# A down projection that takes some of its K tiles two by two by Strassen's scheme

## The chip, the core and the metric

The kernel runs on one core of one Trainium2 chip. TensorE (PE, its weight loads PEld), VectorE (DVE), ScalarE (ACT), GpSimd (POOL) and the DMA queues that SyncE (SP), ACT and POOL issue work side by side and wait for each other by semaphores. The metric is the device time of one execution in microseconds (us); what counts is the median of several runs.

## The reference, cut to what matters

One layer of a diffusion backbone over 256 latent tokens of width 2048 in float32: modulation, a gated linear attention beside a differential attention, a gated merge, and a gated MLP. The change lies in the last product of the MLP and in the residual that follows it.

```python
def conv_ffn(h, w_up, conv_w, conv_b, w_down):
    u = h @ w_up
    ...
    gate, val = jnp.split(u, 2, axis=-1)
    return (jax.nn.silu(gate) * val) @ w_down
...
    x_new = x_new + g2 * conv_ffn(h2_l, w_up, conv_w, conv_b, w_down)
```

`w_down` is 5632 x 2048. The gate `g2` is one vector of 2048, a part of `silu(c) @ w_ada + b_ada`.

## The kernel before

Each float32 operand of a product is split in two parts, hi (rounded to the type that TensorE takes) and lo (the rest); a product is hi x hi + lo x hi + hi x lo, three matmuls into one bank. Weights arrive as 512 KB tiles in `raw` buffers, of which there are four (`fetch`). `split` makes 512 columns of hi by a copy on ACT (`whi`) and of lo by a subtraction on DVE (`wlo`); there are four hi and four lo buffers, so ACT writes a hi when TensorE has left the one four splits earlier. While the up product runs, each fourth lo is made by POOL; in the down product all are DVE's.

The up product makes 44 tiles `g` (`gs[k]`, 128 channels x 256 tokens, lo in `[:, 0]`, hi in `[:, 1]`), each followed by a convolution, silu and gate on ACT and DVE (`gated`). Beside it runs the rest of the modulation vector as dot products on DVE: `ada_next` loads rows of `w_ada` into `araw` (two buffers) and dots them with `cb`, at a pace of so many per up tile; `ada_done(48)` adds up the gate `g2`.

The down product has 256 tokens x 2048 columns. It is made in two halves of 1024 columns (h = 0, 1); a half fills four banks of 128 tokens x 512 columns (t = 0, 1 and n = 0, 1). For each of 44 K tiles k, `pieces(k)` loads 128 x 1024 weights and splits them in two, and `part` does three matmuls for each of the four banks: 12 matmuls per tile and half, 1056 in all, tied in one order. The first half takes the banks named acc, which the up product used last, the second the banks named aux. The last two tiles of the second half are done bank by bank, so that the banks end one after the other.

Between the tiles stand the steps for the residual (`residual`): `gate_line` and a shuffle spread the gate over the partitions into `cb` (POOL DMAs, two shuffles of 1024 columns on DVE); `turn` turns the residual from channels-by-tokens to tokens-by-channels (four transposes on DVE into `turned`, then 32 small POOL DMAs into `row`, four times); `done` multiplies a bank by the gate, adds the row and stores it (two operations on DVE, a store from ACT's queue). `done` for the first half runs in the second.

A scheduler decides the order on each engine: it places instructions by its own costs and may move a step many tiles ahead of where it is written. What one engine does is then in that fixed order, whatever it waits for.

Of the kernel before, what the change touches and what calls it, by code (L numbers as in the profile page):

```python
# [9 lines left out]
F32 = mybir.dt.float32  # L10
F32R = mybir.dt.float32r
# [3 lines left out]
ALU = mybir.AluOpType  # L15
# [3 lines left out]
P = 128  # L19
D = 2048  # L20
T = 256
# [7 lines left out]
FT = FF // P  # L29
# [9 lines left out]
SWW = 32 + C0 + (NGK + 1) * P  # L39
UPS = 6  # L40
CONVS = 7
SLOTS = 12
EARLY_ADA = 4, 14
GATE_ADA = [0.25] * 4 + [0.5] * 16 + [1] * 12
# [102 lines left out]
def layer_kernel(tc, I, out):  # L147
# [3 lines left out]
    with es:  # L151
# [41 lines left out]
        chain = []  # L193
# [31 lines left out]
        def fetch(src, n):  # L225
            raw = st.tile([P, 1024], F32, tag="raw", bufs=4, name="wraw")
            nc.sync.dma_start(raw[:, :n], src)
# [117 lines left out]
        with tc.tile_pool(name="first", bufs=1) as p1:  # L345
# [188 lines left out]
            ws = sweep_splits(0, lows)  # L534
# [663 lines left out]
        with tc.tile_pool(name="ffn", bufs=1) as pf:  # L1198
# [49 lines left out]

            splits[1] = 0
# [15 lines left out]
            def turn(m):  # L1265

                rows.append([hp.tile([P, 512], F32, tag=f"a{4 * t + m}", name="row") for t in range(2)])
                turned = st.tile([P, 1024], F32, tag="araw", bufs=2, name="turned").rearrange("p (c t) -> p c t", c=4)
                for c in range(4):
                    V.transpose(turned[:, c, :], x1[4 * m + c])  # L1270
                for p in range(4):
                    for q in range(8):
                        to = rows[m][q // 4].rearrange("p (c n) -> p c n", c=4)
                        nc.gpsimd.dma_start(to[32 * (q % 4):32 * (q % 4 + 1), :, 32 * p:32 * (p + 1)],  # L1274
                                            turned[32 * p:32 * (p + 1), :, 32 * q:32 * (q + 1)])

            def residual(h, k):

                if (h, k) == (0, 2):
                    V.transpose(gt, adav[:, 32:64])  # L1280
                elif (h, k) in ((0, 3), (0, 4)):
                    lines.append(gate_line(k - 3))
                elif (h, k) in ((0, 14), (0, 15)):
                    V.stream_shuffle(cb[:, 1024 * (k - 14):1024 * (k - 13)], lines[k - 14], [0] * 32)
                elif (h, k) in ((0, 16), (0, 17), (1, 2), (1, 3)):
                    turn(len(rows))
                elif h and 8 <= k < 12:
                    done(0, k % 2, k // 2 % 2)

            lines = []  # L1290
# [6 lines left out]
            def part(t, n, k, w):  # L1297
                ts = slice(t * P, (t + 1) * P)
                g = gs[k]
                for a, b in ((1, 0), (0, 0), (1, 1)):  # L1300
                    i = PE.matmul(banks[h][t][n], g[:, a, ts], w[n][b], start=k == 0 and (a, b) == (1, 0),  # L1301
                                  stop=k == FT - 1 and b == 1)
                    if chain:
                        after(i, chain[0])
                    chain[:] = [i]

            def done(h, t, n, cols=slice(0, 512)):

                o = slice(1024 * h + 512 * n + cols.start, 1024 * h + 512 * n + cols.stop)
                y = hp.tile([P, 512], F32, tag=f"a{8 + (4 * h + 2 * t + n + (cols.start > 0)) % 8}", name="y")[:, :cols.stop - cols.start]  # L1310
                V.tensor_tensor(y, banks[h][t][n][:, cols], cb[:, o], op=ALU.mult)
                V.tensor_tensor(y, y, rows[2 * h + n][t][:, cols], op=ALU.add)
                nc.scalar.dma_start(out[t * P:(t + 1) * P, o], y)

            banks = []
            for h in range(2):
                banks.append([[acc_bank("down") if h == 0 else aux_bank("down", t) for n in range(2)] for t in range(2)])
                last = FT - 2 if h else FT
                for k in range(last):
                    w = pieces(k)  # L1320
                    for n in range(2):
                        for t in range(2):
                            part(t, n, k, w)
                    residual(h, k)

            ws = [pieces(k) for k in range(last, FT)]
            for n in range(2):
                for t in range(2):
                    for k in range(last, FT):
                        part(t, n, k, ws[k - last])  # L1330
# [17 lines left out]
```

## Time and profile before

| | |
|---|---|
| median of 3 runs | 1698.1 us (1697.58 to 1699.21) |
| the profiled execution | 1699.43 us, span 1697.4 us |
| TensorE busy | 1675.4 us (99%) |
| VectorE, ScalarE, GpSimd busy | 1272.3 us (75%), 980.0 us (58%), 329.7 us (19%) |
| weights of the down product | 88 loads of 512 KB, median 4.2 us from issue to landing |
| down product | from 1448.9 us to the end of the span, 1056 matmuls |

The rows of the profile name a line, an engine, an operation and "out<-in"; `xN` counts instructions. A figure in brackets behind an instruction of the timeline is the idle time of its engine before it, with what ended it. A matmul's own duration overlaps the next one's, so its rate is read from start to start.

### The profile page before, as it was taken

How to read it: one execution, taken by the hardware profiler on the slowest of the kernel's cores; microseconds unless marked ns; L12 is line 12 of the kernel's file. 1: busy time of each engine (PE TensorE's matmuls, PEld its weight loads, DVE VectorE, ACT ScalarE, POOL GpSimd, SP SyncE). 2: the span in 40 equal slices, each digit the busy share in tenths (PEclk: the TensorE clock that was granted, in tenths of full speed). 3: DMA queues.
4: the chain of work that ended last, by engine and by line, in shares of the span. 5: the costliest groups of instructions: out<-in, count | busy, mean ns of one | idle time of the engine just before them, and what ended most of it. 6: DMA issues, size and time to landing. Idle time of an engine off the chain costs nothing.

```text
span 1697.4 us, 28584 instructions
## 1 busy us (share of the span) xinstructions
PE 1675.4 (99%) x10108; PEld 1445.0 (85%) x10108; DVE 1272.3 (75%) x2426; ACT 980.0 (58%) x1984; POOL 329.7 (19%) x431
## 2 busy tenths in 40 slices
PE   7999999999999999999999999999999999999998
PEld 5779899998787888888888998888888888788887
DVE  5556765767688888788988797787888787755655
ACT  5324554756355777666766686666666666444443
POOL 0000213131210000001223200222222222594000
PEclk9999999999999999999999999999999999999999
DMA  9996532434566555688787566676767676676664
GB/s 383 408 408 192 164 127 90 139 110 156 180 208 226 174 187 187 206 283 275 264 265 261 181 199 217 217 240 223 237 227 236 223 239 228 196 225 203 221 192 143
DMA packets 110830, 370.82 MB, mean 218 GB/s; under 512 B 14432, under 2 KB 19552, under 8 KB 110688
## 3 DMA queue, kind: packets, MB, share of 16 engines
q1 hardware_dynamic: 102112, 362.51, 63.7%
q10 hardware_dynamic: 4032, 4.37, 0.8%
q0 software_dynamic: 4544, 2.14, 0.6%
q8 instruction: 79, 1.29, 0.3%
q14 instruction: 63, 0.52, 0.1%
HBM read 364.73 MB, written 2.10 MB: 216 GB/s over the span
## 4 chain that ended last, share of the span: by engine, by line
PE 93%; DVE 4%; DMA 2%; ACT 1%; issue 1%; DVEq 0%; ACTq 0%
PE down L1301 14%; PE upg L262 9%; PE upv L262 9%; PE gate L262 7%; PE sweep L350 5%; PE upg L264 5%; PE upv L264 4%; PE gate L264 4%; PE mix L262 4%; PE ab L350 2%; PE mix L264 2%; DMA araw<-in_w_ada 2%; PE pgb L262 2%; PE pga L262 2%; PE dk L313 2%; PE dk L315 2%
## 5 line engine op out<-in xcount | busy, mean ns | idle before, releaser
L206 ACT CAST whi<-wraw 128x512 fp32r<-128x512 f32 (+2 forms) x1004 | 606.8, 608 | 396.8 <-DVE wlo L213 112.3
L213 DVE TENSOR_TENSOR wlo<-wraw,whi 128x512 fp32r<-128x512 f32 (+2 forms) x932 | 637.3, 692 | 232.9 <-ACT whi L206 221.7
L262 PE MATMUL upg<-a,whi 128*128 128x512 f32 x656 | 229.0, 391 | 0.0
L262 PE MATMUL upv<-a,whi 128*128 128x512 f32 x656 | 229.0, 391 | 0.0
L1301 PE MATMUL down<-whi,g 128*128 128x512 f32 x704 | 218.1, 391 | 2.2 <-DVE C L274 2.2
L264 PE MATMUL upv<-a,wlo 128*128 128x256 f32 x656 | 182.8, 280 | 0.0
L264 PE MATMUL upg<-a,wlo 128*128 128x256 f32 x656 | 182.6, 280 | 0.0
L262 PE MATMUL gate<-a,whi 128*128 128x512 f32 x512 | 180.5, 398 | 0.7 <-ACT whi L206 0.7
L213 POOL TENSOR_TENSOR wlo<-wraw,whi 128x512 fp32r<-128x512 f32 x72 | 100.3, 1393 | 387.9 <-ACT whi L206 383.7
L338 DVE CUSTOM_DVE_ANT_0 araw<-araw,cb 128x1024 f32<-128x1024 f32 x128 | 159.7, 1249 | 12.5 <-DMA araw<-in_w_ada 12.4
L1301 PEld LDWEIGHTS down<-whi,g 128*128 128x128 f32 x704 | 132.7, 189 | 30.3 <-DVE C L274 2.6
L262 PEld LDWEIGHTS upv<-a,whi 128*128 128x128 f32 x656 | 122.4, 187 | 26.6
L262 PEld LDWEIGHTS upg<-a,whi 128*128 128x128 f32 x656 | 122.4, 187 | 26.5
L264 PE MATMUL gate<-a,wlo 128*128 128x256 f32 x512 | 140.4, 284 | 0.0
L1301 PE MATMUL down<-wlo,g 128*128 128x512 f32 x352 | 137.5, 391 | 0.0
L264 PEld LDWEIGHTS upv<-a,wlo 128*128 128x128 f32 x656 | 123.9, 189 | 0.5
L264 PEld LDWEIGHTS upg<-a,wlo 128*128 128x128 f32 x656 | 123.9, 189 | 0.5
L262 PEld LDWEIGHTS gate<-a,whi 128*128 128x128 f32 x512 | 94.4, 188 | 20.5 <-ACT whi L206 1.0
L264 PEld LDWEIGHTS gate<-a,wlo 128*128 128x128 f32 x512 | 96.5, 189 | 6.2 <-issue 1.8
L262 PE MATMUL mix<-a,whi 128*128 128x512 f32 x256 | 88.8, 396 | 0.0
L1301 PEld LDWEIGHTS down<-wlo,g 128*128 128x128 f32 x352 | 66.5, 189 | 13.8
L1274 POOL DMA_DIRECT2D row<-turned x128 | 69.3, 550 | 32.4 <-DVE turned L1270 18.3
(351 smaller groups left out, 3401.6 us busy)
## 6 DMA issues: line engine op xcount, KB each, us to landing
wraw<-in_w_up SPq DMA_DIRECT2D x164, 512.0 KB, 4.4
araw<-in_w_ada SPq DMA_DIRECT2D x128, 512.0 KB, 5.0
wraw<-in_w_down SPq DMA_DIRECT2D x88, 512.0 KB, 4.2
ada<-in_w_ad SPq DMA_DIRECT2D x64, 512.0 KB, 10.0
wraw<-in_w_gate SPq DMA_DIRECT2D x64, 512.0 KB, 4.1
wraw<-in_w_in SPq DMA_DIRECT2D x58, 512.0 KB, 4.0
wraw<-in_w_proj SPq DMA_DIRECT2D x32, 512.0 KB, 4.6
wraw<-in_w_out SPq DMA_DIRECT2D x32, 512.0 KB, 4.4
```

Source lines behind the costliest of these rows:

```text
L206: copied[0] = S.copy(hi[:, :n], raw)
L213: i = e.tensor_tensor(lo[:, :n], raw, hi[:, :n].bitcast(F32), op=ALU.subtract)
L262: i = PE.matmul(b.rearrange("p (a b) -> p a b", a=2), whi[:, sl], acts[k], start=first, stop=last)
L264: i = PE.matmul(b[:, T:], wlo[:, sl], acts[k][:, 1, :], start=False, stop=last)
L313: PE.matmul(o, whi[:, sl], hi[k], start=first and j == 0, stop=False)
L315: i = PE.matmul(o, wlo[:, sl], hi[k], start=False, stop=last and j == 1)
L338: i = V.tensor_tensor_reduce(raw, raw, cb[:, q * 1024:(q + 1) * 1024], 1.0, 0.0, op0=ALU.mult, op1=ALU.add, accum_out=ada2[:, j, q:q + 1])
L350: return kept(PE.matmul(*args, **kw))
L1274: nc.gpsimd.dma_start(to[32 * (q % 4):32 * (q % 4 + 1), :, 32 * p:32 * (p + 1)], turned[32 * p:32 * (p + 1), :, 32 * q:32 * (q + 1)])
L1301: i = PE.matmul(banks[h][t][n], g[:, a, ts], w[n][b], start=k == 0 and (a, b) == (1, 0), stop=k == FT - 1 and b == 1)
```

## The change

In four pairs of K tiles (8 and 9, 14 and 15, 20 and 21, 26 and 27) the four blocks of tokens x columns are made with seven products for eight. The tokens (two blocks of 128) and the two tiles of the pair make a 2 x 2 matrix of blocks on the left, the two tiles and the two blocks of 512 columns one on the right. `left` makes four sums of g blocks (S1 to S4), and splits them; it is done once, in the first half, and kept in `shi` and `slo` for the second. `right` loads the pair's two weight tiles three tiles ahead and makes four sums t on DVE. `seven` splits three weight blocks and the four t, and does seven times three matmuls: three products go straight to banks of the half (`own`), four to the other set of banks (p1, p5, p6, p7), where they add up over the four pairs. Three tiles after the last pair `add_others` sums those four banks to what each block is still owed, and `done` adds it. In the second half `prepared` has multiplied that by the gate and added the row before, so that `done` needs two operations there, as it did.

Besides: the first half now accumulates in the aux banks and keeps the acc banks for the four products, the second half the other way round. All four turns stand in the first half (written at tiles 1, 2, 24 and 25), the gate lines at its end (36, 37), the shuffles at tiles 0 and 1 of the second half, `done(0)` at 2 to 5. The dot products beside the up product are paced to end three tiles earlier.

```diff
+PAIRS = [8, 14, 20, 26]
...
-                    ada_next(32 / (FT - CONVS))
+                    ada_next(32 / (FT - CONVS - 3))
...
+            def left(k):
+                i = PAIRS.index(k)
+                g, h = [gs[q].bitcast(F32) for q in (k, k + 1)]
+                ...
+                V.tensor_tensor(x[:, 0], g[:, :, two], h[:, :, two], op=ALU.add)
+                V.tensor_tensor(x[:, 1], x[:, 0], g[:, :, one], op=ALU.subtract)
+                V.tensor_tensor(y[:, 0], g[:, :, one], g[:, :, two], op=ALU.subtract)
+                V.tensor_tensor(y[:, 1], h[:, :, one], x[:, 1], op=ALU.subtract)
+                ...
+                for j, z in enumerate((x, y)):
+                    V.tensor_tensor(z[:, :, 0, :], z[:, :, 0, :], z[:, :, 1, :], op=ALU.add)
+                    split_act(hi[:, 2 * j:2 * j + 2], lo[:, 2 * j:2 * j + 2], z[:, :, 0, :])
+                return hi, lo
+            def right(k):
+                b1, b2 = [fetch(I["w_down"][h, q], 1024) for q in (k, k + 1)]
+                t = [hp.tile([P, 512], F32, tag=f"c{j}", name=f"t{j + 1}") for j in range(4)]
+                V.tensor_tensor(t[0], b1[:, 512:], b1[:, :512], op=ALU.subtract)
+                V.tensor_tensor(t[1], b2[:, 512:], t[0], op=ALU.subtract)
+                V.tensor_tensor(t[2], b2[:, 512:], b1[:, 512:], op=ALU.subtract)
+                V.tensor_tensor(t[3], b2[:, :512], t[1], op=ALU.subtract)
+                return b1[:, :512], b2[:, :512], b2[:, 512:], t
+            def product(b, a, w, first, last):
+                for x, y in ((0, 0), (1, 0), (0, 1)):
+                    i = PE.matmul(b, a[x], w[y], start=first and (x, y) == (0, 0), stop=last and y == 1)
+                    ...
+            def seven(k, ws):
+                first, last = k == PAIRS[0], k == PAIRS[-1]
+                b11, b21, b22, t = ws
+                S_ = [[q[:, j, :] for q in lefts[k]] for j in range(4)]
+                own, (p1, p5), (p6, p7) = banks[h], *others[h]
+                for b, a, w in ((p1, whole(0, k), b11), (own[0][0], whole(0, k + 1), b21), (own[0][1], S_[3], b22),
+                                (p5, S_[0], t[0]), (p7, S_[2], t[2]), (p6, S_[1], t[1]), (own[1][0], whole(1, k + 1), t[3])):
+                    mine = b in (p1, p5, p6, p7)
+                    product(b, a, split(w, 512), mine and first, mine and last)
+            def add_others():
+                ...
+                S.copy(c11, p1)
+                V.tensor_tensor(both, p6, c11, op=ALU.add)
+                V.tensor_tensor(c12, p5, both, op=ALU.add)
+                V.tensor_tensor(c21, p7, both, op=ALU.add)
+                V.tensor_tensor(c22, p5, c21, op=ALU.add)
+            def prepared(t, n):
+                r = adds[1][t][n]
+                V.tensor_tensor(r, r, cb[:, columns(1, n)], op=ALU.mult)
+                V.tensor_tensor(r, r, rows[2 + n][t], op=ALU.add)
...
             def done(h, t, n, cols=slice(0, 512)):
+                if h == 0:
+                    V.tensor_tensor(y, b, r, op=ALU.add)
+                    V.tensor_tensor(y, y, cb[:, o], op=ALU.mult)
+                    V.tensor_tensor(y, y, rows[n][t], op=ALU.add)
+                else:
+                    V.tensor_tensor(y, b, cb[:, o], op=ALU.mult)
+                    V.tensor_tensor(y, y, r, op=ALU.add)
...
+                if h == 0 and k + 5 in PAIRS:
+                    lefts[k + 5] = left(k + 5)
+                if k + 3 in PAIRS:
+                    rights[k + 3] = right(k + 3)
...
-                banks.append([[acc_bank("down") if h == 0 else aux_bank("down", t) for n in range(2)] for t in range(2)])
+                sets = [[[acc_bank("down") for n in range(2)] for t in range(2)],
+                        [[aux_bank("down", t) for n in range(2)] for t in range(2)]]
+                banks.append(sets[1 - h])
+                others.append(sets[h])
```

Where the instructions stand now is shown at three places on DVE. In the rows, `C` are tiles of the up product on their way through the convolution (`upv`, `upg` its banks), `x` and `slo` belong to left, `t` to right, `araw` and `ada` to the dot products, and line numbers of the new kernel are one higher above the down product.

DVE at the end of the up product and the start of the down product; the `wlo` behind the transposes, below, is the first of the down product. Before:

```order
L338 ISA ada_77 128x1
L232 TENSOR_TENSOR g_16522<-C_7240,g_16522 128x256
L274 TENSOR_TENSOR C_7556<-upg,C_7556 128x256
L213 TENSOR_TENSOR wlo<-wraw,whi 128x512 x2
L1212 SCALAR_TENSOR_TENSOR C_7960<-C_7556,vec,C_7960 128x255
L338 ISA araw,ada_77<-araw,cb 128x1024
L338 ISA ada_77 128x1
L213 TENSOR_TENSOR wlo<-wraw,whi 128x512
L1214 SCALAR_TENSOR_TENSOR C_7960<-C_7556,vec,C_7960 128x255
L672 TENSOR_TENSOR adav<-ada_77 128x16
L213 TENSOR_TENSOR wlo<-wraw,whi 128x512
L274 TENSOR_TENSOR C_7758<-upv,C_7758 128x256
```

And now:

```order
L339 ISA ada_77 128x1
L233 TENSOR_TENSOR g_16528<-C_7240,g_16528 128x256
L275 TENSOR_TENSOR C_7556<-upg,C_7556 128x256
L1271 STREAM_TRANSPOSE turned<-C_6178 128x256
L1271 STREAM_TRANSPOSE turned<-C_6289 128x256
L1271 STREAM_TRANSPOSE turned<-C_6569 128x256
L1271 STREAM_TRANSPOSE turned<-C_6846 128x256
L214 TENSOR_TENSOR wlo<-wraw,whi 128x512
L673 TENSOR_TENSOR adav<-ada_77 128x16
L1271 STREAM_TRANSPOSE turned<-C_6960 128x256
L1271 STREAM_TRANSPOSE turned<-C_7240 128x256
L1271 STREAM_TRANSPOSE turned<-C_7442 128x256
```

The last dot product is gone from between the first lo, and two turns have come there, one ahead of the first lo and one behind it.

DVE in the first half, where pair 8 is now (before, between the second and the third turn). Before:

```order
L213 TENSOR_TENSOR wlo<-wraw,whi 128x512 x2
L1270 STREAM_TRANSPOSE turned<-C_6960 128x256
L1270 STREAM_TRANSPOSE turned<-C_7240 128x256
L1270 STREAM_TRANSPOSE turned<-C_7442 128x256
L1270 STREAM_TRANSPOSE turned<-C_7556 128x256
L213 TENSOR_TENSOR wlo<-wraw,whi 128x512 x25
```

And now, from the third product of pair 8 to the first lo of tile 10 and on (t_168.. is the right of pair 8, t_170.. that of pair 14, and the x are left of pair 20):

```order
L214 TENSOR_TENSOR wlo<-wraw,whi 128x512
L233 TENSOR_TENSOR slo<-x,shi 128x256
L1292 TENSOR_TENSOR x<-g_13806,g_13930 128x256
L214 TENSOR_TENSOR wlo<-t_16894,whi 128x512
L214 TENSOR_TENSOR wlo<-t_16896,whi 128x512
L1294 TENSOR_TENSOR x<-g_13806 128x256
L1293 TENSOR_TENSOR x<-x,g_13806 128x256
L214 TENSOR_TENSOR wlo<-t_16895,whi 128x512
L1306 TENSOR_TENSOR t_17057<-wraw 128x512
L214 TENSOR_TENSOR wlo<-t_16897,whi 128x512
L214 TENSOR_TENSOR wlo<-wraw,whi 128x512
L1295 TENSOR_TENSOR x<-g_13930,x 128x256
```

Where 25 lo followed each other, the work for pairs 14 and 20 now stands between the lo of pair 8's products.

DVE in the second half, where the first half's results are finished. Before, at tiles 0 to 4 or so of the second half:

```order
L213 TENSOR_TENSOR wlo<-wraw,whi 128x512 x21
L1311 TENSOR_TENSOR y<-down,cb 128x512 x2
L213 TENSOR_TENSOR wlo<-wraw,whi 128x512
L1312 TENSOR_TENSOR y<-y,row 128x512
L1311 TENSOR_TENSOR y<-down,cb 128x512
L1312 TENSOR_TENSOR y<-y,row 128x512
L1311 TENSOR_TENSOR y<-down,cb 128x512
L213 TENSOR_TENSOR wlo<-wraw,whi 128x512
L1312 TENSOR_TENSOR y<-y,row 128x512
L213 TENSOR_TENSOR wlo<-wraw,whi 128x512
L1312 TENSOR_TENSOR y<-y,row 128x512
L213 TENSOR_TENSOR wlo<-wraw,whi 128x512 x83
```

And now, from the second half's tile 12 (the two lo in the first row) to the third of pair 14's products that are made from t:

```order
L214 TENSOR_TENSOR wlo<-wraw,whi 128x512 x2
L1387 STREAM_SHUFFLE cb<-line 128x1024
L214 TENSOR_TENSOR wlo<-wraw,whi 128x512 x2
L1371 TENSOR_TENSOR y<-y,cb 128x512 x4
L214 TENSOR_TENSOR wlo<-wraw,whi 128x512 x2
L1387 STREAM_SHUFFLE cb<-line 128x1024
L1372 TENSOR_TENSOR y<-y,row 128x512 x2
L214 TENSOR_TENSOR wlo<-wraw,whi 128x512
L1372 TENSOR_TENSOR y<-y,row 128x512 x2
L214 TENSOR_TENSOR wlo<-t_18257,whi 128x512
L214 TENSOR_TENSOR wlo<-t_18259,whi 128x512
L214 TENSOR_TENSOR wlo<-t_18258,whi 128x512
```

Both shuffles, which stood near tile 7 of the first half, and the gate and row of done(0) now stand around the lo of tile 13 and pair 14; the sum of bank and debt (y<-down,add) stays at the start of the second half.

More of the change, by code (lines that the diff above doesn't have):

```diff
@@ L1292, in pieces, with four @@
+            def four(k, ws):
+                for n in range(2):
+                    for t in range(2):
+                        product(banks[h][t][n], whole(t, k), ws[n], k == 0, k == FT - 1)
             def pieces(k):
@@ L1295, in pieces @@
                 return [split(raw[:, n * 512:(n + 1) * 512], 512) for n in range(2)]
[L1297 to L1305, printed above, removed]
@@ new lines, in between @@
+            def between(k):
+                if h == 0 and k in (1, 2, 24, 25):
+                    turn(len(rows))
+                if h == 0 and k == 3:
+                    V.transpose(gt, adav[:, 32:64])
+                if h == 0 and k in (36, 37):
+                    lines.append(gate_line(k - 36))
+                if h == 1 and k in (0, 1):
+                    V.stream_shuffle(cb[:, 1024 * k:1024 * (k + 1)], lines[k], [0] * 32)
+                if h == 1 and 2 <= k < 6:
+                    done(0, k // 2 - 1, k % 2)
+                if h == 0 and k + 5 in PAIRS:
+                    lefts[k + 5] = left(k + 5)
+                if k + 3 in PAIRS:
+                    rights[k + 3] = right(k + 3)
+                if k == PAIRS[-1] + 3:
+                    add_others()
+                if h == 1 and 0 <= k - PAIRS[-1] - 4 < 4:
+                    prepared(*divmod(k - PAIRS[-1] - 4, 2))
@@ L1319, in layer_kernel @@
                 for k in range(last):
[L1320 to L1324, printed above, removed]
+                    if k in PAIRS:
+                        seven(k, rights.pop(k))
+                    elif k - 1 not in PAIRS:
+                        four(k, pieces(k))
+                    between(k)
             ws = [pieces(k) for k in range(last, FT)]
@@ L1329, in layer_kernel @@
                     for k in range(last, FT):
-                        part(t, n, k, ws[k - last])
+                        product(banks[1][t][n], whole(t, k), ws[k - last][n], False, k == FT - 1)
                     for cols in [slice(0, 512)] if not (n and t) else [slice(0, 256), slice(256, 512)]:
```

36 lines of the change are left out of this document (19 added, 17 removed).

## The prediction

> **What bounds the kernel now.** I read the page's busy shares first, then the waits from 1444 us on (the down product starts at 1448.9), then the granted clock there, then single rows.
>
> ```profile
> PE 1675.4 (99%) x10108; PEld 1445.0 (85%) x10108; DVE 1272.3 (75%) x2426; ACT 980.0 (58%) x1984; POOL 329.7 (19%) x431
> ...
> ACT whi L206 <- DVE wlo L213: 110.7, 150, 0.7
> DVE wlo L213 <- ACT whi L206: 102.1, 153, 1.3
> ...
> PE down L1301 <- DVE C L274: 2.2, 1, 2.2
> ...
> 1450.30 0.62 PE L1301 MATMUL down<-whi,g 128*128 128x512 f32 x2
> ...
> 1453.34 0.73 PE L1301 MATMUL down<-whi,g 128*128 128x512 f32 x2 [2.18 <-DVE C L274]
> ...
> 1458.47 0.61 PE L1301 MATMUL down<-whi,g 128*128 128x512 f32 x2
> ...
> 1447.41 1.28 DVE L213 TENSOR_TENSOR wlo<-wraw,whi 128x512 fp32r<-128x512 f32 x2
> ...
> 1448.90 0.63 PE L1301 MATMUL down<-whi,g 128*128 128x512 f32 x2
> ...
> 1450.03 1.23 DVE L338 CUSTOM_DVE_ANT_0 araw<-araw,cb 128x1024 f32<-128x1024 f32 x1 [0.94 <-DMA araw<-in_w_ada]
> ...
> 1452.86 0.42 DVE L274 TENSOR_TENSOR C<-upv,C 128x256 f32<-128x256 f32 x1
> ...
> 1452.00:1454.00 2.00, 0.66 (x3) 1.00 0.17 39
> 1454.00:1456.00 2.00, 2.00 (x7) 0.53 0.68 248
> 1456.00:1458.00 2.00, 2.00 (x7) 0.62 0.65 214
> 1458.00:1460.00 2.00, 2.00 (x10) 1.00 0.19 53
> ```
>
> TensorE is the bound, with DVE and ACT passing work to and fro beneath it. The only wait of TensorE that is listed in the down product is the 2.18 us at 1453: the fourth bank still held the last up product, whose reader (C, line 274) stood on DVE behind a dot product that waited for its load. In the last four rows (stretch, length, PE's busy time and count, granted clock, DMA share, GB/s) the wait is followed by 4 us at 0.53 and 0.62 of the clock. From the matmul at 1450.30 to the one at 1458.47 PE starts 18 matmuls, which I use for the whole price of the wait.
>
> ```profile
> 1599.89 0.62 ACT L206 CAST whi<-wraw 128x512 fp32r<-128x512 f32 x1 [0.74 <-DVE wlo L213]
> 1599.91 0.62 PE L1301 MATMUL down<-whi,g 128*128 128x512 f32 x2
> ...
> 1600.54 0.69 DVE L213 TENSOR_TENSOR wlo<-wraw,whi 128x512 fp32r<-128x512 f32 x1 [0.67 <-ACT whi L206]
> ...
> 1601.25 0.62 ACT L206 CAST whi<-wraw 128x512 fp32r<-128x512 f32 x1 [0.74 <-DVE wlo L213]
> 1601.26 3.05 SPq L227 DMA_DIRECT2D wraw<-in_w_down  x2
> 1601.27 0.62 PE L1301 MATMUL down<-whi,g 128*128 128x512 f32 x2
> ```
>
> This is the rhythm. One split (hi on ACT, lo on DVE) feeds six matmuls, 1.36 us, or 0.227 each. ACT starts when PE leaves the split four back (there are four hi and four lo buffers), and lo is there 0.65 + 0.69 = 1.34 us later; PE reaches it three splits on, 4.08 us, and its lo 0.45 us after that. So a lo may be **3.2 us late** for nothing. By the same rate the 18 matmuls from 1450.30 to 1458.47 (8.17 us) should take 4.08: the wait cost 4.1 us with its slow clock.
>
> **The change, part by part.**
>
> *Matmuls.* Eight times 24 become 21: 24 x 0.227 = **-5.4 us**, all on the path.
>
> *Start.* The first half now accumulates in the aux banks, long free; the reader of the last up bank stands behind no dot product any more, and nobody needs that bank before tile 8. **-4.1 us**, bounds -2.2 (the wait alone) and -4.1; I take 4.1, since the slow rows followed this wait and nothing else.
>
> The Trainium skill (TensorE: Matmul & The Clock Gate, Part 1: The HAM clock gate (the "warmup" mystery)) has the clock halved after an idle window of about 3.4 us. By that rule a wait of 2.18 us leaves the clock alone, the start is worth 2.2, and the sum below would be 4.8 + 1.9 = 6.7, or 1704.8. The trace disagrees: 0.53 and 0.62 stand right behind the wait.
>
> *Denser dot products while up runs.* 32 over 34 tiles for 37: 0.1 us of DVE per tile of some 11 us. DVE was busy 40.5 of 50 us there, PE all of it (first row below), so zero; a gain has no source, and a loss would need DVE to be full.
>
> ```profile
> 1300.00:1350.00 50.00, 50.00 (x291) 44.05 (x290) 40.47 (x71) 32.08 (x64) 12.72 (x10) 1.00 0.70 228
> ...
> 1550.00:1600.00 50.00, 50.00 (x222) 41.40 (x222) 29.89 (x45) 22.70 (x38) 11.71 (x22) 1.00 0.70 220
> ...
> 1571.23 1.28 DVE L1311 TENSOR_TENSOR y<-down,cb 128x512 f32<-128x512 f32 x2
> 1572.43 0.68 DVE L213 TENSOR_TENSOR wlo<-wraw,whi 128x512 fp32r<-128x512 f32 x1
> ...
> 1577.83 1.89 DVE L213 TENSOR_TENSOR wlo<-wraw,whi 128x512 fp32r<-128x512 f32 x3
> 1580.18 0.69 DVE L213 TENSOR_TENSOR wlo<-wraw,whi 128x512 fp32r<-128x512 f32 x1 [0.46 <-ACT whi L206]
> ...
> 1469.67 1.43 DVE L1270 STREAM_TRANSPOSE turned<-C 128x256 f32<-128x256 f32 x4
> 1471.01 0.66 DVE L213 TENSOR_TENSOR wlo<-wraw,whi 128x512 fp32r<-128x512 f32 x1
> 1471.59 1.33 DVE L1284 STREAM_SHUFFLE cb<-line 128x1024 f32<-128x1024 f32 x1
> 1472.80 1.29 DVE L213 TENSOR_TENSOR wlo<-wraw,whi 128x512 fp32r<-128x512 f32 x2
> ...
> 1692.59 0.76 DVE L1311 TENSOR_TENSOR y<-down,cb 128x256 f32<-128x256 f32 x2
> ```
>
> *DVE's new work.* When operations queue, these rows give 0.60 us from start to start at 512 wide (1571.23 to 1572.43 for two), 0.34 at 256 wide (0.76 for two, less one's 0.42), 1.34 for four transposes and 1.21 for a shuffle; where one needs the one ahead of it, some 0.1 more. Added are 108 operations: 24 lo, 32 in left (256 wide), 32 in right, 8 in add_others, 4 and 8 in done and prepared: 76 x 0.60 + 32 x 0.34 = 56 us, on a DVE that has room on average (29.9 busy of 50 at 1550). The average doesn't decide. Inside a pair a split feeds only three matmuls, 0.68 us: three splits ahead are 2.04 us, what a lo may be late shrinks to 2.04 + 0.45 - 1.34 = **1.1 us**, and the splits alone take 0.60 of each 0.68. Three places are then too full.
>
> (a) *First half, start to the end of pair 14.* The order puts all four lefts, two rights and three of the four turns here. From the first lo of the down product to the lo of pair 14's last product, DVE has 38 lo (22.8), nine t (5.4), the 32 operations of left (10.9), eight transposes (2.7), seven operations of the last conv (2.6), three bits for gt (0.5) and some ten dependences (1.0): 45.9 us. The first lo started at 1447.41 before; four transposes are put ahead of it, so 1448.75. DVE reaches the end at 1494.7, and 0.5 later for tile 12's load, on which it stands (as in c): 1495.2. PE starts at 1448.9, passes 24 plain splits (32.6) and 13 products (8.8) and wants that lo 0.45 later, at 1490.8. **+4.4 us.** Bounds: 2.5 (no dependences, no wait for the load, other small operations at half price) and 6.0 (0.64 for each lo). I take the sum of the rows.
>
> (b) *Second half, pair 14.* From the second lo of tile 12 to the lo of the pair's fourth product DVE now has 7 lo (4.2), both shuffles (2.4) and eight operations of done(0) (4.8): 11.4, and 0.1 until it can be used. PE comes to that second split of tile 12 only 1.0 us after DVE starts on it (tile 12 was late, see c), and wants the fourth product's lo 1.36 + 2.72 + 2.04 + 0.45 = 6.6 us after that. So 11.5 - 1.0 - 6.6: **+3.9**. Bounds: 1.5, with the plain lead of 3.4 in place of 1.0, and 3.9. At 1571 the old kernel put eight such operations among plain splits, and PE didn't wait; here the shuffles and a pair are added, so I take the upper end.
>
> (c) *Loads.* A pair k holds two of the four raw buffers from three tiles ahead, so tile k+4 is fetched only when DVE has done the second lo of tile k+2; in the plain rhythm a load has four tiles of time (SP row at 1601.26: a load goes out as a lo ends).
>
> ```profile
> wraw<-in_w_down SPq DMA_DIRECT2D x5, 512.0 KB, 3.3
> ...
> wraw<-in_w_down SPq DMA_DIRECT2D x8, 512.0 KB, 3.6
> ...
> wraw<-in_w_down SPq DMA_DIRECT2D x8, 512.0 KB, 4.3
> ```
>
> Times to landing in 1455:1470, 1490:1510 and 1580:1600; I take the one measured nearest in time, with 3.3 and 4.3 as ends. Second half, pair 8, from its first matmul on: DVE ends the seventh lo at 3.7, stands for the load of tile 15 (issued near 0, landed at 4.3), makes a t by 4.9 and the first lo of tile 10 by 5.6; PE comes to that tile at 4.76 and wants it at 5.2: 0.4 late. A t and the second lo: 6.9. Now tile 12 is fetched, lands at 11.2, and its lo is there 1.34 later at 12.55; PE wants it at 10.65 + 0.4: 1.5 late. So 1.9, the same after pair 20, 1.7 after pair 14 (whose t is ahead); after pair 26 no right follows. First half, pair 20, with 3.6: 0.5. **+6.0**, bounds 1.4 (3.3 everywhere) and 7.5 (4.3 in the first half too).
>
> *Banks of the second half.* add_others reads p1 to p7 three tiles after pair 26, far ahead of tile 0 of the second half: zero, hidden by 14 tiles (38 us). *POOL:*
>
> ```profile
> L1274 POOL DMA_DIRECT2D row<-turned x128 | 69.3, 550 | 32.4 <-DVE turned L1270 18.3
> ...
> out_y<-y ACTq DMA_DIRECT2D x7, 256.0 KB, 2.0
> ```
>
> The 128 row DMAs now come first and the two lines last. The last turn's transposes stand near tile 24 (1515); 32 x 0.55 more and the lines make it about 1550, and the shuffle wants a line near 1600: zero; if a line were late, DVE's lo would queue behind the shuffle and PE behind them. *SP:* the same 88 loads, a pair's two now ahead of the two tiles before it: priced in (c). *ACT:* 34 casts and copies more, some 19 us, at 22.7 busy of 50: zero; the four stores of done(0) stand in ACT's queue between pair 14's casts and wait there for y, but the lo of those casts stand behind the same operations on DVE: part of (b). *Tail:* two operations for a block as before; the last half block takes the y of the first, whose store, three blocks earlier, lands in 2.0: zero.
>
> Sum: -5.4 - 4.1 + 4.4 + 3.9 + 6.0 = **+4.8**. The profiled execution took 1699.43 (span 1697.4 and 2.0 around it), 1.3 above the median of 1698.1; it becomes 1704.2, the median run 1702.9. I say 1703.
>
> **Rivals.** Three runs can tell about 0.2% from no change, 3.4 us, so faster means under 1694.7 and slower over 1701.5.
> - *DVE keeps up* (faster). What decides is the sum of TensorE's waits in the down product against the 9.5 saved: under 6.1 it is faster. If the full stretches (a) and (b) are absorbed, as the burst at 1571 was, and loads cost the middle of their bounds, 4 us, it is 1698.1 - 9.5 + 4 = 1692.6. Against it: that burst had 3.2 us of lead, the pairs have 1.1.
> - *Loads take 3.3 throughout* (same). (c) is 1.4, (a) half a microsecond less: 1698.1 - 9.5 + 3.9 + 3.9 + 1.4 = 1697.8. For it: the late loads go out singly. Against it: so they did at 1600, with 4.3.
> - *The start is worth its wait only* (slower): the slow clock comes anyway, since PE waits for its first los. 1698.1 - 5.4 - 2.2 + 14.3 = 1704.8. Against it: those waits are under 1 us each. The page of the Trainium skill named above gives the same time by its rule.
> - *The clock drops again* (slower): in (b) one product alone waits 2.2 us, as long as the wait at 1453 did. Another 1.9: 1704.8; with a second such place, 1707.
>
> **Chances.** The forecast as summed 0.32, its own range 1701.5 to 1704; the start worth 2.2 only: 0.05; the clock drops again: 0.13; loads fast, or half of (a) and (b) absorbed: 0.33; DVE keeps up: 0.17. So slower 0.50, same 0.33, faster 0.17. With all lower bounds the sum is -9.5 + 2.5 + 1.5 + 1.4 = -4.1, 1694; with all upper ones and a clock drop, 1698.1 - 9.5 + 6.0 + 3.9 + 7.5 + 1.9 = 1707.9: the range.
>
> **What would show it.** Right: no PE wait near 1453 and clock 1.0 there; the up product unchanged; PE waits on wlo (line 214) summing to 12 or more, in pairs 8 and 14 of the first half with DVE busy nine tenths or more; in the second half a cluster at pair 14 behind the shuffles, and ACT whi waiting for DMA at tiles 12, 18 and 24. Wrong: PE whole through pairs 8 and 14, or whi never waiting for a load; wrong the other way: new half-clock stretches, or a shuffle waiting for line.

## The result, and the profile after

The changed kernel takes **1710.15 us** (median of 6 runs, 1708.92 to 1713.11), the kernel before, run beside it, 1699.05 (1697.58 to 1699.40). The ratio on record is 1.0072, with a 95% interval of 1.0062 to 1.0083; these two medians alone give 1.0065. It is slower, by more than was forecast: 1703 was said, with a range from 1694 to 1708. The profiled execution took 1708.92, its span 1706.9, 9.5 more than the span before.

The page's busy times, and the waits from 1447 us on (who waited for whom, us in total, times, longest):

```profile
PE 1677.3 (98%) x10084; PEld 1440.2 (84%) x10084; DVE 1322.6 (77%) x2534; ACT 993.9 (58%) x2018; POOL 327.3 (19%) x431
...
ACT whi L207 <- DMA wraw<-in_w_down: 34.4, 12, 5.7
PEld down L1315 <- DVE wlo L214: 17.4, 20, 2.9
PE down L1315 <- DVE wlo L214: 9.3, 11, 2.5
DVE t L1306 <- DMA wraw<-in_w_down: 6.8, 5, 3.2
```

There are 24 fewer matmuls, and TensorE is nevertheless busy for 1.9 us longer: some of them ran at half clock, and short delays are hidden under the modelled ends of the matmuls before them. Of the 18.5 us that are placed below, 9.3 are listed as waits on wlo. The wait of 2.18 us on C is gone; eleven waits on wlo have come, the longest 2.5. TensorE's own rows over 0.6 us are these six (idle time before the matmul in brackets):

```profile
1477.61 0.50 PE L1315 MATMUL down<-wlo,g 128*128 128x512 f32 x1 [0.63 <-DVE wlo L214]
1488.13 0.50 PE L1315 MATMUL down<-wlo,g 128*128 128x512 f32 x1 [0.79 <-DVE wlo L214]
...
1513.43 0.67 PE L1315 MATMUL down<-wlo,shi 128*128 128x512 f32 x1 [2.50 <-DVE wlo L214]
...
1603.59 0.50 PE L1315 MATMUL down<-wlo,g 128*128 128x512 f32 x1 [0.97 <-DVE wlo L214]
...
1619.32 0.73 PE L1315 MATMUL down<-wlo,shi 128*128 128x512 f32 x1 [1.94 <-DVE wlo L214]
...
1640.31 0.50 PE L1315 MATMUL down<-wlo,shi 128*128 128x512 f32 x1 [1.05 <-DVE wlo L214]
```

To place the whole loss I took the starts of all matmuls of the down product from the trace. Undisturbed, they follow each other every 0.2268 us; what the time from one start to the next has above that is **lateness**, waits and slow clock together. The kernel before has 4.06 us of it, all between 1450.8 and 1457.6. The changed kernel has 18.0 in these places (and 0.5 in crumbs):

| place | forecast | measured |
|---|---|---|
| start of the first half, to the end of pair 14 (1449 to 1496) | (a) 4.4 | 0.8 + 3.7 |
| first half, pair 20 (1510.6 to 1517.2) | (c) 0.5 | **4.4** |
| second half, pair 8 to tile 12 (1600.6 to 1610.0) | (c) 1.9 | 2.0 |
| second half, pair 14 (1615.0 to 1622.9) | (b) 3.9 + (c) 1.7 | 4.7 |
| second half, pair 20 to tile 24 (1638.9 to 1648.6) | (c) 1.9 | 2.4 |
| sum | 14.3 | 18.0 |

It closes: 24 x 0.2268 = 5.4 fewer, 18.5 - 4.0 = 14.5 more lateness, 0.2 before and 0.3 behind the product: 9.6, and the unrounded spans differ by 9.56. The forecast had nearly every place right, and one too low by 3.9 us: the first half's pair 20. DVE's rows there, and loads by the time they were sent (count, size, median us to landing; first those of 1504 to 1508.5, then those of 1480 to 1500):

```profile
1507.55 1.37 DVE L214 TENSOR_TENSOR wlo<-t,whi 128x512 fp32r<-128x512 f32 x2 [0.67 <-PE down L1315]
1512.08 0.69 DVE L1306 TENSOR_TENSOR t<-wraw 128x512 f32<-128x512 f32 x1 [3.16 <-DMA wraw<-in_w_down]
1512.69 1.29 DVE L214 TENSOR_TENSOR wlo<-t,whi 128x512 fp32r<-128x512 f32 x2
...
wraw<-in_w_down SPq DMA_DIRECT2D x3, 512.0 KB, 6.3
...
wraw<-in_w_down SPq DMA_DIRECT2D x7, 512.0 KB, 3.7
```

Between the second and the third lo of pair 20 that are made from t stands a t of pair 26 on DVE. It stood 3.16 us for tile 26's load. The two lo behind it needed nothing from that load; TensorE waited 2.5 us for the first of them and then ran at half clock till 1517. The load was sent at 1505.6, with two others within 1.9 us, and landed at 1512.0.

In the second half the shuffles and the end of done(0) stand on DVE around pair 14 as the order had it, and a lo that TensorE wants waits behind them:

```profile
1610.15 1.32 DVE L1387 STREAM_SHUFFLE cb<-line 128x1024 f32<-128x1024 f32 x1
1611.36 1.28 DVE L214 TENSOR_TENSOR wlo<-wraw,whi 128x512 fp32r<-128x512 f32 x2
1612.56 2.49 DVE L1371 TENSOR_TENSOR y<-y,cb 128x512 f32<-128x512 f32 x4
1614.96 1.29 DVE L214 TENSOR_TENSOR wlo<-wraw,whi 128x512 fp32r<-128x512 f32 x2
...
1616.18 1.31 DVE L1387 STREAM_SHUFFLE cb<-line 128x1024 f32<-128x1024 f32 x1
1617.38 1.28 DVE L1372 TENSOR_TENSOR y<-y,row 128x512 f32<-128x512 f32 x2
1618.57 0.69 DVE L214 TENSOR_TENSOR wlo<-wraw,whi 128x512 fp32r<-128x512 f32 x1
```

### The profile page after: what moved, and what is told of

Same layout as the page of the kernel before. It is cut to its first block, busy times and chain, and to the rows that moved or that the text cites. A ratio compares the mean times of both kernels' runs of the same rounds, so it can differ in the third digit from the quotient of the medians.

```text
span 1706.9 us, 28735 instructions
## 1 busy us (share of the span) xinstructions
PE 1677.3 (98%) x10084; PEld 1440.2 (84%) x10084; DVE 1322.6 (77%) x2534; ACT 993.9 (58%) x2018; POOL 327.3 (19%) x431
## 4 chain that ended last, share of the span: by engine, by line
PE 88%; DVE 5%; DMA 4%; issue 1%; ACT 1%; DVEq 0%; SPq 0%; ACTq 0%
PE down L1315 10%; PE upg L263 9%; PE upv L263 9%; PE gate L263 7%; PE sweep L351 5%; PE upv L265 5%; PE upg L265 5%; PE gate L265 4%; PE mix L263 3%; DVE wlo L214 2%; PE ab L351 2%; DMA wraw<-in_w_down 2%; PE mix L265 2%; PE pgb L263 2%; PE pga L263 2%; PE dk L314 2%
## 5 line engine op out<-in xcount | busy, mean ns | idle before, releaser
L207 ACT CAST whi<-wraw 128x512 fp32r<-128x512 f32 (+2 forms) x996 | 598.6, 608 | 382.9 <-PE upg L263 77.2
L214 DVE TENSOR_TENSOR wlo<-wraw,whi 128x512 fp32r<-128x512 f32 (+2 forms) x924 | 626.9, 691 | 181.1 <-ACT whi L207 170.6
L1315 PE MATMUL down<-whi,g 128*128 128x512 f32 x624 | 194.1, 392 | 0.2
L1315 PEld LDWEIGHTS down<-whi,g 128*128 128x128 f32 x624 | 117.6, 189 | 25.4 <-ACT whi L207 1.4
L1315 PE MATMUL down<-wlo,g 128*128 128x512 f32 x312 | 123.3, 395 | 3.6 <-DVE wlo L214 3.6
L1315 PEld LDWEIGHTS down<-wlo,g 128*128 128x128 f32 x312 | 58.9, 189 | 20.8 <-DVE wlo L214 8.8
```

The lines of the kernel that those rows point to most:

```text
L207: copied[0] = S.copy(hi[:, :n], raw)
L214: i = e.tensor_tensor(lo[:, :n], raw, hi[:, :n].bitcast(F32), op=ALU.subtract)
L1315: i = PE.matmul(b, a[x], w[y], start=first and (x, y) == (0, 0), stop=last and y == 1)
```

## The experiments

The theory: the lateness has four causes, each with its place. The start was one event, wait and slow clock. The t of a next pair stand on DVE for loads ahead of lo that are ready. The shuffles and done(0) stand ahead of pair 14. Lefts and turns fill DVE in the first pairs. The main rival is that the pairs leave DVE too little room, so that moved work comes back as waits elsewhere. Ratios are to the kernel before, run beside each.

**The banks alone.** The kernel before, with its two halves' banks exchanged:

```
-banks.append([[acc_bank("down") if h == 0 else aux_bank("down", t) for n in range(2)] ...
+banks.append([[acc_bank("down") if h == 1 else aux_bank("down", t) for n in range(2)] ...
```

> The kernel before with one edit: the first half of the down product accumulates in the aux banks, the second half in the acc banks. No product of blocks is saved, no operation added. Theory (the wait for the fourth bank and the four half-clock microseconds behind it are one event, 4.06 us by the excess of its matmuls over 0.2268 us each): 1699.05 - 4.1 = 1695.0. First rival (only the wait of 2.18 us goes, the slow clock comes anyway): 1696.9. Second rival (TensorE waits at the start for its first lo instead): 1698 to 1699.

Measured: 1695.31 against 1697.87, ratio 0.9985 (0.9976 to 0.9994), so 1.0 to 4.1 us less: the times exclude neither the theory nor the first rival. The traces tell more. The first and last start of the product's first kind of matmul, of the kernel before and of this one:

```profile
L1301 PE MATMUL down<-whi,g x704: 387/389/628, 1448.9 to 1691.9; 128*128 128x512 f32 x176
```

```profile
L1301 PE MATMUL down<-whi,g x704: 387/389/397, 1452.2 to 1691.1; 128*128 128x512 f32 x176
```

243.0 us became 238.9, with no matmul over 397 ns: lateness 4.06 became 0. (This profiled execution came 3.2 us late to the product, by two half-clock stretches at 463.5 and 538.6 us, in work that the edit does not touch.) Between these two executions the start was worth 4.1, wait and slow clock as one.

In the medians it was worth 2.6, and the granted clocks on record show a reason. Of 43 executions of the kernel before that ran beside the experiments, 24 have a mean granted clock of 1.000, and one stretch of 3.41 us at half clock would take 0.001 off that. So in those 24 the clock did not drop behind the wait. Ten of the 22 beside this run are such; their median is 1697.46, 2.2 above this kernel's 1695.31, about what the wait alone took. How long the wait was in those executions no trace shows.

**Shuffles, late turns and done(0) among plain tiles.** The gate lines early, the shuffles at tiles 17 and 18 of the first half:

```
-if h == 0 and k in (36, 37): lines.append(gate_line(k - 36))
-if h == 1 and k in (0, 1):   V.stream_shuffle(cb[:, 1024 * k:...], lines[k], [0] * 32)
+if h == 0 and k in (4, 5):   lines.append(gate_line(k - 4))
+if h == 0 and k in (17, 18): V.stream_shuffle(cb[:, 1024 * (k - 17):...], lines[k - 17], [0] * 32)
```

The last two turns and done(0) are written where they were. In the order that came of it they stand among plain tiles too, at 1536 to 1545 and 1571 to 1582.

> The changed kernel with the two gate lines made early, so that the shuffles, the last two turns and all twelve operations of done(0) stand on DVE among plain tiles, none of them in the second half's pair 14. Theory (the 4.7 us that TensorE loses at that pair are the shuffles and done(0) ahead of its lo): the pair loses what its neighbours 8 and 20 lose, 2.0 to 2.4, and the loss of 1.1 behind the third turn (1487) goes too: 1710.15 - 2.5 - 1.0 = 1706.6. Rival (the pair is late through its loads, and the shuffles only stand where DVE has to wait anyway): 1709 to 1710. Second rival (shuffles and turns cost the same in their new place, behind pair 26): 1710.

Measured: 1704.49, ratio 1.0041 (1.0028 to 1.0053). Lateness at the second half's pair 14 fell from 4.7 to 1.7, and the 1.1 behind the third turn went, as the theory had it; the burst of done(0) costs 1.1 in its new place and tiles 22 to 25 of the first half 1.3. Another 2.8 came from pair 20 of the first half, which no theory had foretold. There the same t waited again, for loads that took 4.8 us in place of 6.3, and TensorE's wait of 1.33 us was not followed by a slow clock:

```profile
1510.16 0.69 DVE L1306 TENSOR_TENSOR t<-wraw 128x512 f32<-128x512 f32 x1 [2.00 <-DMA wraw<-in_w_down]
...
1511.51 0.50 PE L1315 MATMUL down<-wlo,shi 128*128 128x512 f32 x1 [1.33 <-DVE wlo L214]
...
wraw<-in_w_down SPq DMA_DIRECT2D x3, 512.0 KB, 4.8
```

**Loads in their natural order.** right one tile ahead of the pair, so that no buffer is held out of turn:

```
-if k + 3 in PAIRS: rights[k + 3] = right(k + 3)
+if k + 1 in PAIRS: rights[k + 1] = right(k + 1)
```

> The changed kernel with the right sums of a pair (and its two loads) written one tile ahead of the pair, where they were written three tiles ahead: tiles are loaded in the order 8, 9, 10, 11 again, and no buffer is held out of turn. Theory (loads held back by the pair's two buffers, and t operations that stand on DVE for loads sent in a bunch): the losses at the first half's pair 20 (4.4), and at the second half's pairs 8 (2.0) and 20 (2.4) go, and 1 to 2 of the 4.7 at pair 14: 1710.15 - 8.8 - 1.5 = 1700, within 1698 to 1702. Rival (DVE is too full within a pair: the four t, 2.4 us, now stand closer to the pair's own seven lo and make them late): 1706 to 1712.

Measured: 1697.68, ratio 0.9999 (0.9990 to 1.0008). The lateness at the first half's pair 20 and at the second half's pairs 8 and 20 is gone entirely; pair 14 keeps 4.35, 0.4 less than in the changed kernel. 3.4 stay up to pair 14 of the first half. The waits of this kernel are worth a look:

```profile
DVE t L1307 <- DMA wraw<-in_w_down: 6.8, 7, 1.6
DVE t L1306 <- DMA wraw<-in_w_down: 5.8, 7, 1.6
PE down L1315 <- DVE wlo L214: 4.9, 6, 1.5
```

DVE stands for loads *longer* than in the changed kernel (12.6 us against 8.5), and nothing is lost any more at those three places: the lo behind those t belong to plain tiles and may be 3.2 us late, not 1.1. The fastest kernel below shows it without anything else beside it: there DVE stands 14.3 us for loads in front of t, and no matmul of the product is late.

**DVE's order alone.** The four t of each right may not be put ahead of what is written before them:

```
-V.tensor_tensor(t[0], b1[:, 512:], b1[:, :512], op=ALU.subtract)
+tc.keep_in_program_order(V.tensor_tensor(t[0], b1[:, 512:], b1[:, :512], op=ALU.subtract))
...  (t[1], t[2], t[3] alike)
```

> The changed kernel with one edit: the t of the next pair may not be put on DVE ahead of the lo that are written before them, so none stands for its load between the lo of the pair before. Loads and buffers are as in the changed kernel. Theory (TensorE's wait of 2.5 us in the first half's pair 20 and of 1.05 in the second half's are t operations standing for a load in front of a lo that was ready to run): 4.4 + 1.7 go, and the 1.2 at the second half's tile 10: 1710.15 - 7 = 1703. Rival (the loads are late however DVE is ordered, and the waits go to the tiles behind the pair): 1707 to 1710.

Measured: 1703.41, ratio 1.0034 (1.0021 to 1.0046). The time is as the theory said, by a path that it did not foresee: the first half's pair 20 and the second half's pairs 14 and 20 lose nothing any more (0.5 at tile 19 is left), but the order now puts a shuffle, all eight operations of done(0) and three t in a row ahead of the second half's pair 8:

```profile
1590.96 1.31 DVE L1390 STREAM_SHUFFLE cb<-line 128x1024 f32<-128x1024 f32 x1
1592.30 2.50 DVE L1374 TENSOR_TENSOR y<-y,cb 128x512 f32<-128x512 f32 x4
1594.71 2.49 DVE L1375 TENSOR_TENSOR y<-y,row 128x512 f32<-128x512 f32 x4
1597.12 0.68 DVE L1309 TENSOR_TENSOR t<-wraw 128x512 f32<-128x512 f32 x1
...
1598.58 0.79 PE L1318 MATMUL down<-whi,shi 128*128 128x512 f32 x1 [5.31 <-ACT whi L207]
```

That place loses 9.5 us with its slow clock, where pair 8 lost 2.0 and pair 14 4.7. As this edit moved more than it should, a smaller one followed.

**Four operations.** The same for the t of the first half's pair 26 only (`if (h, k) == (0, 23)` around it):

> The changed kernel with the smallest edit: only the four t of the first half's pair 26 may not be put on DVE ahead of what is written before them; loads, buffers and all other work as in the changed kernel. Theory (the first t stands on DVE for a load of 6.4 us, and behind it stand the last two lo of pair 20, which were ready to run; TensorE waits 2.5 us for them and then runs at half clock): the 4.37 us lost at that pair go, and nothing else changes: 1710.15 - 4.4 = 1705.8, ratio to the kernel before 1.0047. Rival (the three loads sent within 2 us make everything behind them late): part of the wait comes back at tiles 22 to 24 or at pair 26, 1707.5 to 1710.

Measured: 1706.54, ratio 1.0057 (1.0044 to 1.0071). The interval overlaps with the changed kernel's (1.0062 to 1.0083), so the times alone do not tell the two apart; the trace does. Lateness between 1497 and 1597 is 0, where it was 4.4, and no other place moved by more than 0.7. Together the other places lost 1.6 more, so that the sum fell by 2.8, from 18.5 to 15.7, and not by 4.4; with one trace of each kernel it stays open whether that is the edit or spread. The loads are as slow as ever; the four lo run through, and the t find their load landed:

```profile
1508.61 2.73 DVE L214 TENSOR_TENSOR wlo<-t,whi 128x512 fp32r<-128x512 f32 x4 [0.67 <-PE down L1318]
1511.33 2.73 DVE L214 TENSOR_TENSOR wlo<-wraw,whi 128x512 fp32r<-128x512 f32 x4
1513.98 0.69 DVE L1309 TENSOR_TENSOR t<-wraw 128x512 f32<-128x512 f32 x1
...
wraw<-in_w_down SPq DMA_DIRECT2D x3, 512.0 KB, 6.2
```

So the slow loads as such cost nothing at this pair; four t in the wrong place made them cost 4.4 us. The rival is out: nothing came back at tiles 22 to 24 or at pair 26.

This trace shows one thing more. It has no half-clock stretch in the product, yet the second half's pair 14 loses 4.2 us, and 0.7 more at the tiles behind it, where the changed kernel lost 4.7 with its clock at half from 1619.4. There DVE's order holds TensorE back at either clock, and the second drop cost nothing that these traces tell.

**Both edits, natural loads and early lines:**

> Both edits at once: right one tile ahead of the pair, gate lines early. Theory (the two losses are separate: DVE's t standing for loads on the one hand, shuffles and done(0) ahead of pair 14 on the other): of the 7.9 us that TensorE still loses in the down product with the first edit, the 4.4 at the second half's pair 14 go; some 2.5 in the first half's pairs 8 and 14 and 0.8 at the start stay: about 4.2 under the first edit alone, some 0.6 to 1.2 back for the burst of done(0) in its new place, so ratio to the kernel before about 0.998, 1694.5 where before takes 1697.9. Rival (DVE lacks room as such in the pairs, and moved work comes back as waits elsewhere): no better than with the first edit alone, ratio 1.000.

Measured: 1693.41 against 1698.07, ratio 0.9965 (0.9951 to 0.9979): faster than the kernel before. Lateness 1.9 in all: 0.8 at the start, 1.1 in the first two pairs, none in the second half. The theory had left some 4 us and a ratio of 0.998, so it had the gain too small. Moved work did not come back.

**Pairs later:** `PAIRS = [14, 20, 26, 32]` on top of both:

> The same two edits, and the four pairs at tiles 14, 20, 26, 32 in place of 8, 14, 20, 26: DVE has six more plain tiles (16 us) for the four lefts and the first turns before a pair comes. Theory (the loss of 2.5 us in the first pairs of the first half is DVE's queue of lefts and turns): it goes, and only the 0.8 at the start and under 1 near pair 32 (a shuffle and two turns) stay: ratio 0.9965 (1692 where before takes 1697.9). Rival (a pair loses some half microsecond wherever it stands, since a lo there may be only 1.1 us late): as the kernel of both edits, 0.998.

Measured: 1694.04, ratio 0.9972 (0.9960 to 0.9983). The interval holds both the theory's 0.9965 and the rival's 0.998. In the trace the lateness of the first pairs went as the theory had it, but the last pair now meets both shuffles and two turns and loses 2.0, not under 1: there the theory missed.

**First turns behind tiles 3 and 5** on top of that (`k in (3, 5, 24, 25)` for the turns, held in program order; gt at 6, lines at 7 and 8):

> The kernel with later pairs, and the first two turns pinned behind tiles 3 and 5, so that no transposes stand on DVE ahead of the first lo of the down product. Theory (the 0.8 us lost at 1450 are the first lo behind eight transposes): another 0.6 to 0.8 us less than with later pairs alone, 1691.3 where before takes 1697.9. Rival (the first lo are late through their loads, which landed at 1447 to 1449): no change.

Measured: **1691.16** against 1698.07, ratio 0.9955 (0.9943 to 0.9968), the fastest of all. Lateness is 0, at the start and everywhere. The time that was said, 1691.3, was met by luck: it was 0.7 under a kernel of later pairs at 1692, which took 1694.0. The 0.8 of the start went as the theory had it; 2.0 went besides, since the pinned turns and the shuffles now stand behind pair 32 and leave it alone. Its first and last start:

```profile
L1318 PE MATMUL down<-whi,g x624: 387/390/398, 1448.2 to 1681.8; 128*128 128x512 f32 x156
```

233.6 us, against 238.9 with the banks alone: the saved products are worth 5.3 (5.43 from the first to the very last matmul), and the start 4.1.

**Two pairs** (14 and 26) in the kernel of later pairs:

> The kernel with later pairs, but only the pairs at 14 and 26: half of the saved products (12 matmuls fewer where the other has 24), half of the left, right and extra lo operations. Theory (each saved product of three matmuls is worth 0.68 us once no lo is late): 2.7 us more than with four pairs. Rival (the four pairs give back in small waits what they save): equal to four pairs, or faster.

Measured: 1693.54, ratio 0.9973 (0.9962 to 0.9983), no slower than the four pairs of 1694.04: the rival, in that kernel, since its last pair gave back 2.0. In the traces the price of a product holds: from first to last matmul 237.3 us with a lateness of 0.8, against 233.8 with none, so 2.7 for two pairs in each half.

## Why the prediction was wrong, and where it was right

- *Matmuls, -5.4:* right; 5.43 between two kernels without lateness.
- *Start, -4.1:* right for the profiled execution, where wait and slow clock went as one; too much for the median, where the banks alone gave 2.6. That the clock drops behind this wait was taken as given, and in 24 of 43 executions it did not.
- *(a), 4.4:* right; 4.5, in four steps of 0.8, 1.4, 1.6 and 0.7 as DVE fell behind. It went step by step with its causes: 1.0 with the third turn, the rest with the t, the lefts' place and the first turns.
- *(b), 3.9:* right in its cause: 0 with both edits, shuffles and done(0) elsewhere. The stretch on DVE, from the second lo of tile 12 to the fourth product's, took 11.5 us (1609.5 to 1621.1), as added up. The 4.35 with loads in order is no proof of the size, since there the pair's own t stand in the same stretch.
- *(c), second half:* 1.9, 1.7 and 1.9 were said, 2.0, 0.4 and 2.4 came. The sizes are near, their make-up is not: tile 12's late load, said to be worth 1.5, cost 0.6; the t that stands for a load cost 1.4 and 1.75, where 0.4 was said. That the sums agree is luck.
- *(c), first half, "pair 20, with 3.6: 0.5":* **this step failed.** It measured 4.4. The 3.6 us to landing came from 1490 to 1510 of the old kernel, where loads went out one by one; here three went out within 1.9 us and took 5.8 to 6.4. With 3.6 the load, sent at 1505.6, would have landed at 1509.2, and DVE came to the t at 1508.9: 0.3. With 6.4 DVE stood 3.16, TensorE 2.5, and the slow clock that followed took another 1.7. The order of t and lo was there to be read; that the t in the middle of the pair has two ready lo behind it with 1.1 us to spare was not put together with a load that is slow. Why these loads were slow stays open (see the end); that the order made them cost 4.4 is shown by the run with four operations pinned.
- *Banks, POOL, SP, ACT, tail, denser dot products, 0:* right within 0.3 before and behind the product. The second line had landed at 1561.4 (said: about 1550), the first shuffle ran at 1610.
- *Signs:* TensorE's waits on wlo were to sum to 12 or more; 9.3 are listed, and the rest of the lateness is slow clock and delays too short to be listed. New half-clock stretches, named as a sign that more is lost, came.
- *Rivals:* "the clock drops again" was given 0.13 and priced at 1707 for two places, 1.9 each. It came twice, at 1513.6 and 1619.4: the first cost 1.7, the second nothing that can be told. The failed step adds 3.9 to the forecast's 4.8, with the first of these drops in it; the other places, the crumbs and the two edges add 0.8: 9.5, what the spans show. The medians differ by 11.1, 1.6 more, because the profiled execution of the changed kernel is the fastest of its six, 1.2 under their median, and that of the kernel before lies 0.4 above its own. What the slower executions lost no trace here shows.

## What to carry to other kernels

Where an in-order engine may stand for a transfer, ask what is queued behind that operation and how late *that* may be: 14.3 us of such waits were free in the fastest kernel, 3.2 us in the middle of a pair cost 4.4. Don't price a transfer by the median of the old rhythm alone: ask what the order costs when the load is slow. A price read from one profiled execution, a clock drop above all, need not be the median's. A saving on the bound engine is there to be had once the work that pays for it stands where there is slack: the same change that cost 11 us in one order gained 7 in another, 5.4 of it by the saved products between the traces.

## What the runs showed of the hardware

The granted clock changes on a grid. Stretches of 3.41 us, the first two of the kernel before, the others of the changed one (length, busy time and count of PE, PEld, DVE, ACT, POOL, then the granted clock):

```profile
1450.70:1454.12 3.42, 1.24 (x5) 0.69 (x5) 3.42 (x11) 1.22 (x4) 0.95 (x1) 1.00 0.37 123
1454.12:1457.53 3.41, 3.41 (x9) 2.63 (x8) 2.08 (x5) 1.52 (x3) 2.79 (x5) 0.50 0.61 211
```

```profile
1510.19:1513.60 3.41, 0.91 (x5) 0.45 (x4) 1.52 (x3) 0.81 (x3) 0.00 (x0) 1.00 0.17 65
1513.60:1517.02 3.42, 3.42 (x9) 2.68 (x10) 3.42 (x7) 1.09 (x2) 0.00 (x0) 0.50 0.00 0
...
1616.00:1619.42 3.42, 1.48 (x7) 0.86 (x6) 3.42 (x7) 1.05 (x3) 0.00 (x0) 1.00 0.65 205
1619.42:1622.83 3.41, 3.19 (x7) 2.08 (x8) 3.41 (x7) 1.19 (x3) 0.00 (x0) 0.50 0.97 266
```

Each time here the clock is at half for just one such stretch, and the two drops of the changed kernel lie 105.8 us apart, 31 of them. In the stretch before the drop TensorE was busy for only a part, 0.91, 1.24 and 1.48 us of 3.41. In the kernel of four operations a wait of 1.96 us, as long as the 1.94 here, was followed by no drop. With the grid laid back from where that execution's clock next changes (1701.6, 25 stretches on), its wait is cut in two, and the stretch has 1.65 busy; so had the run with DVE's order alone one of 1.56, at full clock behind it:

```profile
1612.87:1616.28 3.41, 1.65 (x6) 1.05 (x6) 3.41 (x6) 1.24 (x2) 0.00 (x0) 1.00 0.54 167
1616.28:1619.69 3.41, 2.33 (x9) 1.63 (x10) 3.41 (x7) 1.60 (x3) 0.00 (x0) 1.00 0.99 272
```

```profile
1591.71:1595.12 3.41, 1.56 (x7) 0.95 (x6) 3.38 (x6) 0.00 (x0) 0.00 (x0) 1.00 0.00 0
1595.12:1598.54 3.42, 0.00 (x0) 0.00 (x0) 3.39 (x7) 0.62 (x1) 0.00 (x0) 1.00 0.66 250
1598.54:1601.95 3.41, 2.85 (x5) 1.33 (x5) 3.41 (x6) 2.28 (x4) 0.00 (x0) 0.50 0.62 215
```

So within the down product the border lies between 1.48 and 1.56 busy of 3.41. It is no rule for the whole kernel: far ahead of the product, at other matmuls, the clock fell after 1.59 in the run with the banks alone:

```profile
535.17:538.58 3.41, 1.59 (x7) 1.00 (x7) 2.50 (x7) 1.78 (x5) 0.00 (x0) 1.00 0.51 139
538.58:541.99 3.41, 3.41 (x8) 2.23 (x8) 3.41 (x8) 1.65 (x4) 0.00 (x0) 0.50 0.73 252
```

In that run it also fell after 1.86 (460.08 to 463.49). So no one share of this modelled busy time parts the falls from the rest: after 1.56 and 1.65, above, it stayed. In the product, whether a wait of some 2 us trips the clock depends on where it falls, and whether the drop then costs another 1.7 depends on whether TensorE or DVE holds the work up. Nor does a drop always last one stretch: with DVE's order alone it lasted two (6.83 us), the first of them with 2.85 busy. The Trainium skill (TensorE: Matmul & The Clock Gate, Part 1: The HAM clock gate (the "warmup" mystery)) has a free-running window of 3.4 us; length and grid agree with the rows above. That a whole window must be idle does not: a window with 1.48 us of 3.41 busy, 43%, was followed by the drop.

Three loads of 512 KB sent within 1.9 us took 5.8 to 6.4 us to land, where the seven of 1480 to 1500 had a median of 3.7. That they went out together is not shown to be the cause: three sent within 2.2 us from 1489.0 took 3.5 to 4.7, and in the kernel before one load, sent at 1647.5 and 2.7 us ahead of the next, took 6.2. With the gate lines early the same three took 4.7 to 5.4. The queue of the small row transfers used 9.5% of the DMA engines' time from 1504 to 1508.5 in the changed kernel and 0.7% at the same loads with the gate lines early; no run separates that from the rest, and what made the loads slow stays open.
